# The softmax scaling of the mixers' attention maps moved from VectorE to GpSimd

## The chip, the cores and the metric

The kernel runs on one core of one Trainium2 chip. The core has five engines that run at the same time and wait for each other with semaphores: TensorE (PE, matrix products; its weight loads are shown apart as PEld), VectorE (DVE), ScalarE (ACT), GpSimd (POOL) and SyncE (SP, which issues the DMA transfers). The metric is the device time of the whole program in microseconds (us), the median of several runs.

## The reference

The program is a two-layer backbone over 256 context tokens and 256 latent tokens of width 1024. Each layer is a half-weighted SwiGLU feed-forward part, a mixer, and a second feed-forward part, with modulated RMS norms in front of each. The mixer runs three kinds of heads beside each other on one input projection and joins them in one output projection:

```
# differential heads (4 of them, two maps each)
s1 = q1 @ k1^T * SCALE ; s2 = q2 @ k2^T * SCALE
p  = softmax(s1) - lam * softmax(s2)
o  = rms_norm(p @ v, subln_g) * (1 - lam_init)

# grouped-query heads (4 query heads on 2 key heads)
p  = softmax(q @ k^T)
o  = p @ v

# a bidirectional gated linear recurrence on 256 channels
```

The latent queries attend to all 512 tokens. In the first layer the context queries attend to the 256 context tokens as well; in the last layer the context's outputs aren't needed and are left out. All is in float32.

## The kernel before

Activations are kept transposed, features on the 128 partitions and the 512 tokens along the row. A product of two float32 matrices is made of three TensorE products (`mm3`, lines 375 to 377): each operand is split into a high part (rounded, ScalarE) and a low part (the rest, VectorE, line 369). The two feed-forward parts of each layer take most of the time; the mixers lie at about 410 to 610 us (layer 0) and 1370 to 1530 us (layer 1) of the span.

In the mixer an attention map is computed for 128 queries at a time, queries on the partitions and keys along the row, 256 or 512 of them. `scores` (line 698) has TensorE write the scores to one of three PSUM banks. `softmax` (line 704) has VectorE take the negative maximum of each row (L706), ScalarE the exponential with the row sums as by-product (the call in line 708, shown in the profile as L86, the helper that records it), and VectorE the reciprocal of the sum (L709). The exponentials lie in one of five buffers `e`, the small columns (maximum, sum, reciprocal, scaled reciprocal) in one of eight tiles `sm`.

- In `gqa_att` (line 721) the exponentials are multiplied by the reciprocals (L728) and go to `to_keys`.
- In `da_att` (line 770) there are two maps. The second one's reciprocal is first multiplied by minus lambda (L776), then the second map's exponentials by that (L777), and one instruction scales the first map and adds the second (L778: two tensors in, one out). The sum goes to `to_keys`.
- `to_keys` (line 712) transposes the map in blocks on TensorE (L717) into a single PSUM bank, and ScalarE copies it out (L718). The products with the values follow on TensorE (L734, L783).

Between these steps TensorE works on projections of later heads (`m0vp`, `m0q3p`, `m0k3p` and the like) and on the output projection (`m0oy`), as far as their inputs are there. `rope` (line 521) rotates queries and keys: a shuffle on VectorE (L524), a product with the sine table on GpSimd (L525), one with the cosine table on VectorE (L526), and the sum on VectorE (L527). `stack_q` and `stack_k` split the rotated tensors into their parts (L641, L651, L652 on ScalarE, L642 and L653 on VectorE), `subln` normalises the differential heads (L798 to L804), and `take_m` splits finished heads for the output projection (L790 on ScalarE, L791 on VectorE).

The order of the heads is written in lines 827 to 851. The order of the instructions on each engine is made by a scheduler when the program is built: it takes the instructions by priority as their inputs become ready by its own estimates of durations, and fixes one list per engine. Each engine then works through its list in order, so an instruction that waits holds up all that stand behind it on its engine. GpSimd's list holds little: the rotations, some products of the recurrence (L599), sums of squares (L282) and memsets.

Of the kernel before, what the change touches and what calls it, by code (L numbers as in the profile page):

```python
# [13 lines left out]
ALU = mybir.AluOpType  # L14
# [44 lines left out]
def hybrid_kernel(ctx: ExitStack, tc, x, c, ctx_tok, c_ctx, ada_w, ada_b, norm_g, ffn1_w13, ffn1_w2,  # L59
# [3 lines left out]
    V, S, G, PE = nc.vector, nc.scalar, nc.gpsimd, nc.tensor  # L63
# [32 lines left out]
    def ps(name="ps", tag="ms"):  # L96
        return pss.tile([128, 512], F32, tag=tag, name=name)
# [431 lines left out]
    def mixer(l, c0, nstat):  # L529
        W = w_in[l]  # L530
        nm = f"m{l}"
        with tc.tile_pool(name=f"mp{l}", bufs=1) as mp, tc.tile_pool(name=f"mt{l}", bufs=1) as mt:
            def m512(name, dtype=F32, tag="T"):
                return mt.tile([128, 512], dtype, tag=tag, name=f"{nm}{name}", bufs=TAGS[tag])
# [163 lines left out]
            def scores(q, k, u, a, nk):  # L698
                s = acc_bank(1, "s")
                PE.matmul(s[:, 0:nk], q[u][:, a:a + 128], k[u][:, 0:nk], start=True, stop=False)  # L700
                PE.matmul(s[:, 0:nk], q[u][:, a:a + 128], k[2 + u][:, 0:nk], start=False, stop=True)  # L701
                return s

            def softmax(s, nk, name):
                st_ = sml.tile([128, 4], F32, tag="sm", name="sm", bufs=8)
                V.reduce_max(st_[:, 0:1], s[:, 0:nk], axis=AX.X, negate=True)  # L706
                e = m512(name, tag="e")
                tabled(e[:, 0:nk], s[:, 0:nk], AF.Exp, bias=st_[:, 0:1], accum_out=st_[:, 1:2])
                V.reciprocal(st_[:, 2:3], st_[:, 1:2])  # L709
                return e, st_  # L710

            def to_keys(p, nk):

                tp = ps("tp", "tp")
                pT = m512("pT", tag="p")
                for kt in range(nk // 128):
                    PE.transpose(tp[:, 128 * kt:128 * kt + 128], p[:, 128 * kt:128 * kt + 128], ident)  # L717
                S.activation(pT[:, 0:nk], tp[:, 0:nk], AF.Copy)  # L718
                return pT

            def gqa_att(hp, q0, nk):
                n = nk // 128
                pTs = []
                for qt in range(2):
                    for u in range(2):
                        s = scores(gqa[u], gqa[2], hp, q0 + 128 * qt, nk)
                        e, st_ = softmax(s, nk, "e")
                        V.tensor_scalar(e[:, 0:nk], e[:, 0:nk], st_[:, 2:3], None, op0=ALU.mult)  # L728
                        pTs.append(to_keys(e, nk))
                o = ps("o")  # L730
                for qt in range(2):
                    for kt in range(n):
                        for u in range(2):
                            PE.matmul(o[64 * u:64 * u + 64, 128 * qt:128 * qt + 128],  # L734
                                      gvs[0][:, 128 * kt + 64 * hp:128 * kt + 64 * hp + 64],
                                      pTs[2 * qt + u][:, 128 * kt:128 * kt + 128], start=(kt == 0), stop=(kt == n - 1))
                if 4 + hp not in om:
                    om[4 + hp] = m512(f"og{hp}", tag="o")
                S.activation(om[4 + hp][:, q0:q0 + 256], o[:, 0:256], AF.Copy)
# [30 lines left out]
            def da_att(h, q0, nk):  # L770
                n = nk // 128
                pTs = []
                for qt in range(2):
                    es = [softmax(scores(dq[h], dk[h], u, q0 + 128 * qt, nk), nk, f"e{u}") for u in range(2)]
                    (e1, s1), (e2, s2) = es
                    V.tensor_tensor(out=s2[:, 3:4], in0=s2[:, 2:3], in1=nlam[:, l:l + 1], op=ALU.mult)  # L776
                    V.tensor_scalar(e2[:, 0:nk], e2[:, 0:nk], s2[:, 3:4], None, op0=ALU.mult)  # L777
                    V.scalar_tensor_tensor(e1[:, 0:nk], e1[:, 0:nk], s1[:, 2:3], e2[:, 0:nk], op0=ALU.mult, op1=ALU.add)  # L778
                    pTs.append(to_keys(e1, nk))
                o = ps("o")  # L780
                for qt in range(2):
                    for kt in range(n):
                        PE.matmul(o[:, 128 * qt:128 * qt + 128], vs[h // 2, kt // 2][:, 256 * (kt % 2) + 128 * (h % 2):256 * (kt % 2) + 128 * (h % 2) + 128],  # L783
                                  pTs[qt][:, 128 * kt:128 * kt + 128], start=(kt == 0), stop=(kt == n - 1))
                if h not in om:
                    om[h] = m512(f"o{h}", tag="o")
                S.activation(om[h][:, q0:q0 + 256], o[:, 0:256], AF.Copy)
# [41 lines left out]
            qk_head(1, raw)  # L829
            gqa_proj()  # L830
            attend(da_att, 0)
            attend(da_att, 1)
            gqa_norm()
            ws = v_split(1)
            for t in range(4):
                v_tile(1, ws, t)
            subln((0, 1))
            attend(gqa_att, 0)
            raw = qk_load(1)
            qk_head(2, raw)  # L840
            attend(gqa_att, 1)
            attend(da_att, 2)
            qk_head(3, raw)
            attend(da_att, 3)
# [149 lines left out]
```

## Time and profile before

| | us |
|---|---|
| median of 3 runs | 1734.68 |
| lowest and highest run | 1734.53, 1737.2 |
| the profiled execution | 1734.71 |
| its span in the trace | 1732.9 |

| engine | busy us | share of the span |
|---|---|---|
| TensorE | 1694.8 | 98% |
| VectorE | 1211.4 | 70% |
| ScalarE | 709.6 | 41% |
| GpSimd | 76.4 | 4% |

A busy time counts an instruction from its start to its end. Matmuls are pipelined and their ends are modelled, so short gaps between them do not show. In the rows below a line "L728 DVE" is line 728 on VectorE; "out<-in" names the tiles, with the number of partitions and elements; the share of a slice or window tells how full an engine is while it matters, which the share over the whole span doesn't.

### The profile page before, as it was taken

The numbers are of one execution on the slowest core, as the hardware profiler recorded it, in microseconds if no ns is written. First come the engines' busy times: TensorE is split into PE (matmuls) and PEld (weight loads), VectorE is DVE, ScalarE is ACT, GpSimd is POOL, SyncE is SP. The second block draws the span as 40 slices with busy tenths as digits, with TensorE's granted clock in tenths as the row PEclk, the third lists the DMA queues.
The fourth block names the chain that finished last, engine by engine and source line by source line (L and its number), as shares of the span: only waits on it lengthen the run. The fifth ranks groups of instructions, "written<-read, shape, count | busy, mean of one in ns | idle before, by whom it ended". The sixth has DMA issues, their size and how long they took to land.

```text
span 1732.9 us, 22954 instructions
## 1 busy us (share of the span) xinstructions
PE 1694.8 (98%) x9245; PEld 1440.7 (83%) x9245; DVE 1211.4 (70%) x1863; ACT 709.6 (41%) x1116; POOL 76.4 (4%) x75
## 2 busy tenths in 40 slices
PE   6999999999999999999999999999999999999998
PEld 3788888889787798888888888888888988799997
DVE  5798994337579869999696494563333778987574
ACT  4422222224677743221223342222222477865354
POOL 0000000011101010000000100000001110010001
PEclk9999999999999999999999999999999999999999
DMA  9665752233211147667464344333322332145552
GB/s 347 208 233 203 240 173 98 85 110 104 73 50 50 49 144 245 228 207 244 148 218 163 104 146 146 110 109 98 97 81 90 106 119 74 59 159 179 189 177 92
DMA packets 192817, 249.27 MB, mean 144 GB/s; under 512 B 6722, under 2 KB 170952, under 8 KB 192712
## 3 DMA queue, kind: packets, MB, share of 16 engines
q1 hardware_dynamic: 192712, 247.82, 42.9%
q8 instruction: 72, 1.18, 0.3%
q14 instruction: 33, 0.27, 0.0%
HBM read 246.75 MB, written 1.05 MB: 143 GB/s over the span
## 4 chain that ended last, share of the span: by engine, by line
PE 90%; DVE 6%; ACT 2%; issue 1%; DMA 0%; POOL 0%; SPq 0%; ACTq 0%; DVEq 0%; POOLq 0%
PE f_0pb L377 5%; PE f_0pb L375 5%; PE f_0pb L376 5%; PE f_0pa L376 5%; PE f_0pa L375 5%; PE f_0pa L377 5%; PE f_2pb L376 4%; PE f_2pb L377 4%; PE f_2pa L375 4%; PE f_2pb L375 4%; PE f_2pa L377 3%; PE f_2pa L376 3%; PE f_0w0y L375 3%; PE f_0w0y L377 3%; PE f_0w0y L376 3%; PE f_2w0y L375 2%
## 5 line engine op out<-in xcount | busy, mean ns | idle before, releaser
L227 DVE SCALAR_TENSOR_TENSOR aacc<-araw,cpad,aacc 128x1024 f32<-128x1024 f32 x224 | 276.8, 1279 | 0.0
L86 ACT ACTIVATE g<-f_0pa 128x512 f32<-128x512 f32 x44 | 26.3, 598 | 150.2 <-PE f_0pa L377 150.2
L282 POOL TENSOR_TENSOR sss<-sss,sqs 128x512 f32<-128x512 f32 (+1 forms) x20 | 27.5, 1377 | 1281.5 <-ACT sqs L280 1281.5
L515 DVE TENSOR_TENSOR g<-g,f_0pb 128x512 f32<-128x512 f32 x44 | 30.2, 686 | 68.3 <-PE f_0pb L377 68.0
L369 DVE TENSOR_TENSOR f_0w_0L<-f_0w,f_0w_0H 128x1024 fp32r<-128x1024 f32 (+1 forms) x32 | 34.9, 1090 | 53.5 <-ACT f_0w_0H L368 53.3
L368 ACT ACTIVATE f_0w_0H<-f_0w 128x1024 fp32r<-128x1024 f32 (+1 forms) x32 | 30.5, 952 | 91.9 <-PE f_0w0y L377 43.7
L368 ACT ACTIVATE f_2w_0H<-f_2w 128x1024 fp32r<-128x1024 f32 (+1 forms) x32 | 30.5, 953 | 69.1 <-PE f_2w0y L377 30.7
L369 DVE TENSOR_TENSOR f_2w_0L<-f_2w,f_2w_0H 128x1024 fp32r<-128x1024 f32 (+1 forms) x32 | 34.9, 1089 | 29.1 <-ACT f_2w_0H L368 28.9
L375 PE MATMUL f_0w0y<-f_0gH,f_0w_0H 128*128 128x512 f32 x128 | 50.2, 392 | 0.0
L377 PE MATMUL f_0w0y<-f_0gL,f_0w_0H 128*128 128x512 f32 x128 | 49.9, 390 | 0.0
L376 PE MATMUL f_0w0y<-f_0gH,f_0w_0L 128*128 128x512 f32 x128 | 49.8, 389 | 0.0
L706 DVE TENSOR_REDUCE sm<-s 128x1 f32<-128x512 f32 (+1 forms) x72 | 41.8, 588 | 5.8 <-PE s L701 5.7
L317 ACT ACTIVATE xH<-xn,mods 128x256 fp32r<-128x256 f32 x80 | 35.4, 499 | 25.6 <-DVE xn L316 25.5
L375 PE MATMUL f_2w0y<-f_2gH,f_2w_0H 128*128 128x512 f32 (+1 forms) x128 | 43.2, 338 | 0.0
L377 PE MATMUL f_2w0y<-f_2gL,f_2w_0H 128*128 128x512 f32 (+1 forms) x128 | 43.1, 336 | 0.0
L376 PE MATMUL f_2w0y<-f_2gH,f_2w_0L 128*128 128x512 f32 (+1 forms) x128 | 43.0, 336 | 0.0
L369 DVE TENSOR_TENSOR f_0w_4L<-f_0w,f_0w_4H 128x1024 fp32r<-128x1024 f32 x16 | 19.5, 1221 | 33.0 <-ACT f_0w_4H L368 33.0
L375 PE MATMUL f_0w1y<-f_0gH,f_0w_0H 128*128 128x512 f32 (+1 forms) x120 | 41.7, 348 | 0.0
L376 PE MATMUL f_0w1y<-f_0gH,f_0w_0L 128*128 128x512 f32 (+1 forms) x120 | 41.6, 347 | 0.0
L377 PE MATMUL f_0w1y<-f_0gL,f_0w_0H 128*128 128x512 f32 (+1 forms) x120 | 41.6, 346 | 0.0
L86 ACT ACTIVATE g<-f_2pa 128x512 f32<-128x512 f32 x22 | 13.2, 599 | 68.1 <-PE f_2pa L377 68.1
L368 ACT ACTIVATE f_0w_4H<-f_0w 128x1024 fp32r<-128x1024 f32 x16 | 17.0, 1061 | 58.6 <-PE f_0w0y L377 25.8
(1382 smaller groups left out, 5878.6 us busy)
## 6 DMA issues: line engine op xcount, KB each, us to landing
araw<-in_ada_w_dram SPq DMA_DIRECT2D x64, 1024.0 KB, 4.9
f_0a<-in_ffn_w_dram SPq DMA_DIRECT2D x22, 1024.0 KB, 7.2
f_0b<-in_ffn_w_dram SPq DMA_DIRECT2D x22, 1024.0 KB, 6.1
f_2a<-in_ffn_w_dram SPq DMA_DIRECT2D x22, 1024.0 KB, 7.6
f_2b<-in_ffn_w_dram SPq DMA_DIRECT2D x22, 1024.0 KB, 5.1
f_0w<-in_ffn_w_dram SPq DMA_DIRECT2D x16, 1024.0 KB
f_2w<-in_ffn_w_dram SPq DMA_DIRECT2D x16, 1024.0 KB, 5.3
adas<-in_ada_w_dram SPq DMA_DIRECT2D x16, 512.0 KB, 7.7
```

The costliest lines, as they stand in the source:

```text
L86: i = S.activation(out_, in_, func, **kw)
L227: V.scalar_tensor_tensor(acc[:, v], w[:, i], cpad[:, k, v:v + 1], acc[:, v], op0=ALU.mult, op1=ALU.add)
L282: adder.tensor_tensor(out=self.sum[:, a:b], in0=self.sum[:, a:b], in1=sq[:, a:b], op=ALU.add)
L317: S.activation(xH[:, k, a:b], t[:, a:b], AF.Identity, bias=sh)
L368: S.activation(vH, src, AF.Copy)
L369: V.tensor_tensor(out=vL, in0=src, in1=f32(vH), op=ALU.subtract)
L375: PE.matmul(acc, aH, bH, start=first, stop=False)
L376: PE.matmul(acc, aL, bH, start=False, stop=False)
L377: PE.matmul(acc, aH, bL, start=False, stop=last)
L515: V.tensor_tensor(out=t_[:, c0:], in0=t_[:, c0:], in1=pb[:, c0:], op=ALU.mult)
L706: V.reduce_max(st_[:, 0:1], s[:, 0:nk], axis=AX.X, negate=True)
```

## The change

Two instructions are issued on GpSimd (`G`) instead of VectorE (`V`), with the same operands: the scaling of the grouped-query exponentials, and that of the second differential map.

```
@@ -725,7 +725,7 @@
                     for u in range(2):
                         s = scores(gqa[u], gqa[2], hp, q0 + 128 * qt, nk)
                         e, st_ = softmax(s, nk, "e")
-                        V.tensor_scalar(e[:, 0:nk], e[:, 0:nk], st_[:, 2:3], None, op0=ALU.mult)
+                        G.tensor_scalar(e[:, 0:nk], e[:, 0:nk], st_[:, 2:3], None, op0=ALU.mult)
                         pTs.append(to_keys(e, nk))
                 o = ps("o")
                 for qt in range(2):
@@ -774,7 +774,7 @@
                     es = [softmax(scores(dq[h], dk[h], u, q0 + 128 * qt, nk), nk, f"e{u}") for u in range(2)]
                     (e1, s1), (e2, s2) = es
                     V.tensor_tensor(out=s2[:, 3:4], in0=s2[:, 2:3], in1=nlam[:, l:l + 1], op=ALU.mult)
-                    V.tensor_scalar(e2[:, 0:nk], e2[:, 0:nk], s2[:, 3:4], None, op0=ALU.mult)
+                    G.tensor_scalar(e2[:, 0:nk], e2[:, 0:nk], s2[:, 3:4], None, op0=ALU.mult)
                     V.scalar_tensor_tensor(e1[:, 0:nk], e1[:, 0:nk], s1[:, 2:3], e2[:, 0:nk], op0=ALU.mult, op1=ALU.add)
                     pTs.append(to_keys(e1, nk))
                 o = ps("o")
```

24 instructions of each kind move: in layer 0 sixteen of each (eight with 256 keys, eight with 512), in layer 1 eight of each, all with 512. The scheduler makes new lists from it, so other instructions of the mixers change their places too; SyncE's list stays the same.

VectorE in the first differential heads of layer 0 before: the second maps' scaling (L777) and the sum that uses it (L778), `m0e_3721` and `m0e_3747` being second maps with 512 keys.

```order
L777 TENSOR_SCALAR m0e_3721<-m0e_3721,sm 128x512
L709 RECIPROCAL sm<-sm 128x1
L706 TENSOR_REDUCE sm<-s 128x1
L778 SCALAR_TENSOR_TENSOR m0e_3713<-m0e_3713,sm,m0e_3721 128x512
L776 TENSOR_TENSOR sm<-sm,nlam 128x1
```

The same place of VectorE now, from the scaled reciprocal of the first of these maps on.

```order
L776 TENSOR_TENSOR sm<-sm,nlam 128x1
L709 RECIPROCAL sm<-sm 128x1
L706 TENSOR_REDUCE sm<-s 128x1 x2
L778 SCALAR_TENSOR_TENSOR m0e_3713<-m0e_3713,sm,m0e_3721 128x512
L709 RECIPROCAL sm<-sm 128x1 x2
```

L777 has gone from VectorE's list, and between the scaled reciprocal and the sum stand two maxima here, elsewhere one.

GpSimd in layer 0's mixer: before, the eleven rotation products stand there alone; now the multiplications stand between them. One piece of the difference, from the seventh rotation on.

```order
+L525 TENSOR_TENSOR sh<-sh,cs 128x256 x3
+L728 TENSOR_SCALAR m0e<-m0e,sm 128x256 x3
+L525 TENSOR_TENSOR sh<-sh,cs 128x256
+L728 TENSOR_SCALAR m0e<-m0e,sm 128x256
+L728 TENSOR_SCALAR m0e<-m0e,sm 128x512 x2
+L525 TENSOR_TENSOR sh<-sh,cs 128x256
+L728 TENSOR_SCALAR m0e<-m0e,sm 128x512 x2
+L525 TENSOR_TENSOR sh<-sh,cs 128x256
+L728 TENSOR_SCALAR m0e<-m0e,sm 128x256 x4
```

A rotation now waits in line behind one to three multiplications, each of which waits for a reciprocal from VectorE.

VectorE in layer 0's grouped-query part now, where the rotation and stacking of the next head (`m0qr`, `m0Q`, `kz`) stand among the maxima and reciprocals of the maps.

```order
L706 TENSOR_REDUCE sm<-s 128x1
L642 TENSOR_TENSOR m0Q_4267<-m0qr,m0Q_4267 64x512
L653 TENSOR_TENSOR kz_2951<-m0qr,m0K_4308 64x512
L524 STREAM_SHUFFLE sh<-m0qr 128x256
L526 TENSOR_TENSOR sh<-m0qr,cs 128x256
L369 TENSOR_TENSOR m0o_0_4L<-m0o_0_4819,m0o_0_4H 128x1024
L653 TENSOR_TENSOR kz_2952<-m0qr,m0K_4309 64x512
L709 RECIPROCAL sm<-sm 128x1
L527 TENSOR_TENSOR m0qr<-sh 128x256
```

Before, the same head's instructions stood there with the multiplications L728 between them. L526, L527, L642, L653 and L369 each read two tensors.

## Rows read from the trace of the kernel before

**Rows 1.** The page: busy us of each engine (share of the span) and instructions.
```profile
PE 1694.8 (98%) x9245; PEld 1440.7 (83%) x9245; DVE 1211.4 (70%) x1863; ACT 709.6 (41%) x1116; POOL 76.4 (4%) x75
```

**Rows 2.** The page: the chain of work that ended last, shares by engine.
```profile
PE 90%; DVE 6%; ACT 2%; issue 1%; DMA 0%; POOL 0%; SPq 0%; ACTq 0%; DVEq 0%; POOLq 0%
```

**Rows 3.** VectorE's groups of one shape: xcount | busy us, mean ns | idle before.
```profile
L728 DVE TENSOR_SCALAR m1e<-m1e,sm 128x512 f32<-128x512 f32 x8 | 4.7, 597 | 0.0
L728 DVE TENSOR_SCALAR m0e<-m0e,sm 128x512 f32<-128x512 f32 x8 | 4.2, 535 | 0.0
L777 DVE TENSOR_SCALAR m1e<-m1e,sm 128x512 f32<-128x512 f32 x8 | 3.8, 481 | 0.0
L777 DVE TENSOR_SCALAR m0e<-m0e,sm 128x512 f32<-128x512 f32 x8 | 3.8, 476 | 0.0
L777 DVE TENSOR_SCALAR m0e<-m0e,sm 128x256 f32<-128x256 f32 x8 | 2.8, 345 | 0.0
L728 DVE TENSOR_SCALAR m0e<-m0e,sm 128x256 f32<-128x256 f32 x8 | 2.7, 343 | 0.0
```

**Rows 4.** Mixer windows: width, busy us of PE, PEld, DVE, ACT, POOL; clock; DMA.
```profile
540.00:580.00 40.00, 36.73 (x244) 26.00 (x242) 36.80 (x105) 36.72 (x91) 3.12 (x4) 1.00 0.01 2
1460.00:1520.00 60.00, 57.12 (x392) 47.43 (x392) 53.37 (x125) 46.82 (x97) 5.62 (x7) 1.00 0.28 89
```

**Rows 5.** TensorE's waits, 540 to 580 us: us in total, times, longest.
```profile
PE o L783 <- ACT m0pT L718: 1.6, 2, 0.9
PE m0oy L375 <- ACT xH L790: 1.0, 1, 1.0
PE s L700 <- ACT m0e L86: 0.3, 1, 0.3
```

**Rows 6.** GpSimd's groups of one shape, columns as in rows 3.
```profile
L525 POOL TENSOR_TENSOR sh<-sh,cs 128x256 f32<-128x256 f32 x22 | 19.2, 875 | 211.6 <-DVE sh L524 190.1 <-DVE sm L776 16.0 <-DVE sm L709 5.6
L599 POOL TENSOR_TENSOR m0r<-m0r,m0xc 128x512 f32<-128x512 f32 x4 | 5.1, 1274 | 20.0 <-ACT m0r L86 20.0
L633 POOL MEMSET kz<- 64x512 f32 x8 | 4.2, 521 | 0.4
L554 POOL MEMSET bd<- 128x1024 f32 x2 | 1.9, 955 | 35.2 <-DVE srs L252 35.2
```

**Rows 7.** Layer 0 near 547 us: start us, us, engine, instruction [idle before].
```profile
545.04 0.44 DVE L524 STREAM_SHUFFLE sh<-m0qr 128x256 f32<-128x256 f32 x1
545.38 1.34 DVE L728 TENSOR_SCALAR m0e<-m0e,sm 128x512 f32<-128x512 f32 x2
545.63 0.81 POOL L525 TENSOR_TENSOR sh<-sh,cs 128x256 f32<-128x256 f32 x1 [12.55 <-DVE sh L524]
547.30 0.47 DVE L728 TENSOR_SCALAR m0e<-m0e,sm 128x512 f32<-128x512 f32 x1
547.69 0.41 DVE L526 TENSOR_TENSOR sh<-m0qr,cs 128x256 f32<-128x256 f32 x1
548.62 0.76 POOL L525 TENSOR_TENSOR sh<-sh,cs 128x256 f32<-128x256 f32 x1 [2.18 <-DVE sh L524]
548.70 0.95 DVE L526 TENSOR_TENSOR sh<-m0qr,cs 128x256 f32<-128x256 f32 x1
```

**Rows 8.** Layer 1 near 1481 us, columns as in rows 7.
```profile
1481.07 0.76 POOL L525 TENSOR_TENSOR sh<-sh,cs 128x256 f32<-128x256 f32 x1 [1.93 <-DVE sh L524]
1481.15 0.68 DVE L706 TENSOR_REDUCE sm<-s 128x1 f32<-128x512 f32 x1
```

**Rows 9.** VectorE's row maxima, columns as in rows 3.
```profile
L706 DVE TENSOR_REDUCE sm<-s 128x1 f32<-128x512 f32 x48 | 32.3, 677 | 2.6 <-PE s L701 2.5
L706 DVE TENSOR_REDUCE sm<-s 128x1 f32<-128x256 f32 x24 | 9.5, 410 | 3.3 <-PE s L701 3.2
```

More of the change, by code (lines that the diff above doesn't have):

```diff
@@ L727, in gqa_att @@
                         e, st_ = softmax(s, nk, "e")
-                        V.tensor_scalar(e[:, 0:nk], e[:, 0:nk], st_[:, 2:3], None, op0=ALU.mult)
+                        G.tensor_scalar(e[:, 0:nk], e[:, 0:nk], st_[:, 2:3], None, op0=ALU.mult)
                         pTs.append(to_keys(e, nk))
@@ L776, in da_att @@
                     V.tensor_tensor(out=s2[:, 3:4], in0=s2[:, 2:3], in1=nlam[:, l:l + 1], op=ALU.mult)
-                    V.tensor_scalar(e2[:, 0:nk], e2[:, 0:nk], s2[:, 3:4], None, op0=ALU.mult)
+                    G.tensor_scalar(e2[:, 0:nk], e2[:, 0:nk], s2[:, 3:4], None, op0=ALU.mult)
                     V.scalar_tensor_tensor(e1[:, 0:nk], e1[:, 0:nk], s1[:, 2:3], e2[:, 0:nk], op0=ALU.mult, op1=ALU.add)
```

## The prediction

> **What bounds the kernel now.** I read the busy times first. TensorE is busy 98% of the span, VectorE 70%, ScalarE 41%, GpSimd 4% [rows 1]: nearly all of the time is TensorE's own work, which the change leaves alone. The chain that ended last says the same, 90% TensorE and 6% VectorE [rows 2]. So the change is worth what it does to TensorE's idle time in the two mixers, and nothing elsewhere.
>
> Next, the lines that move. The 48 multiplications take 4.7 + 4.2 + 3.8 + 3.8 + 2.8 + 2.7 = 22.0 us of VectorE: 11.6 us in the grouped-query part (L728: 6.9 in layer 0, 4.7 in layer 1), 10.4 us for the second map (L777) [rows 3]. 22 us is 1.3% of the span, but it is VectorE's time, not TensorE's.
>
> Then the stretches where these lines crowd. From 540 to 580 us (layer 0's grouped-query part and the head after it) VectorE is busy 36.80 of 40 us, ScalarE 36.72, and TensorE idles 3.27. From 1460 to 1520 us (layer 1, a longer stretch) VectorE is busy 53.37 of 60, ScalarE 46.82, and TensorE idles 2.88 [rows 4]. Both helpers are nearly full in layer 0, so an emptied VectorE finds ScalarE next. TensorE's waits in layer 0's stretch all end on ScalarE: on the copy of the transposed map (1.6 us), on a part of the output projection's input (1.0), on an exponential (0.3) [rows 5]. These are late partly because VectorE fed them late, so part of the idle time, not all, is VectorE's to give back. The visible idle time of the two stretches, 3.27 + 2.88 = 6.15 us, is my upper end for a gain. TensorE's spans overlap and hide small gaps, so it is not a strict limit.
>
> **The price of one multiplication on GpSimd.** No row of before shows it. From below, GpSimd's memset, which reads nothing, takes 521 ns for 512 elements and 955 for 1024, so some 0.30 us for 256. From above, its multiplication of two tensors takes 1274 ns for 512 elements; its 256-element one averages 875 [rows 6] and takes 0.76 to 0.81 where it runs in the mixers [rows 7]. The operation added here reads one tensor and a column, so it should lie between; I take 0.90 us for 512 and 0.53 for 256, the middle of the two ends. The 16 short and 32 long ones (the context stream's maps are 256 wide, in layer 0 alone) then make 16 x 0.53 + 32 x 0.90 = 37 us of GpSimd, from 21 to 53 at the ends. GpSimd has that time: it is busy 3.12 of the 40 us [rows 4].
>
> By the Trainium skill, GPSIMD Engine Reference, section 4.1, elementwise work belongs on VectorE, GpSimd being about twice as slow with two inputs and roughly at line rate with one; its section 3.1 gives 769 ns for 512 elements in a tight loop. No row here shows that figure; with it the forecast below would fall by about half a microsecond.
>
> **The grouped-query part, step by step.** Removed: 11.6 us of VectorE. Added: on VectorE nothing, but GpSimd stands in its way. While GpSimd multiplied for 0.76 us from 548.62, VectorE's L526 (two tensors read) took 0.95 us, against 0.41 a microsecond earlier with GpSimd idle; the two L728 around 545.6 took 1.34 together [rows 7], against two times 0.47. So an instruction that meets a running GpSimd loses about 0.5 us. The maxima L706 don't: one ran beside GpSimd at 1481.15 in 0.68 us [rows 8], its usual 677 ns [rows 9].
>
> The Trainium skill (SBUF — State Buffer, "Who interferes with whom") says why the two differ: a VectorE instruction with two tensors in SBUF, or in a two-port mode, shares a port pair with GpSimd, and whoever comes first holds it for the whole instruction; a reduction doesn't. The rows agree. By that rule only the two-tensor instructions below can be hit, and it is the rule that speaks against this change.
>
> In the order of the changed kernel 12 such instructions (L526, L527, L642, L653, L369, L791) stand among layer 0's grouped-query maxima and 13 in layer 1. GpSimd would be busy there about 0.56 of the time (layer 0: 8 x 0.53 + 8 x 0.90 + 3 rotations of 0.8 = 13.9 of some 24.5 us). 25 x 0.56 x 0.5 = 7.0 us; some three of these, 1.4 us, are L526 that meet their own rotation today, as the one at 548.70 did. New: 5.6. VectorE's net relief is 11.6 - 5.6 = 6.0 us. The longer way from the reciprocal through GpSimd to the transpose (0.90 plus two handovers of about 0.1, against 0.47) is covered as long as TensorE has the scores and projections of m0k3 and m1k3 in between; both orders run three to four maps ahead there. Without that cover it would be 24 x 0.5 = 12 us.
>
> GpSimd's queue gets a new neighbour: the rotation products L525 now stand between the multiplications, and VectorE's L527 waits for each. Behind L527 stand the maxima. A rotation that comes behind one or two multiplications is 0.5 to 1.8 us later; L706 and L709 stand in between and take about that, so I cost it at nothing, and at up to 7 x 0.5 us if they don't cover it.
>
> **The differential part.** Removed: 24 L777, 0.48 us (512) or 0.35 (256) each [rows 3]. Added: L778 now waits for GpSimd, with VectorE's next maxima and reciprocals queued behind it, and ScalarE's next exponentials waiting for those. The handover from VectorE to GpSimd takes about 0.15 us (L524 ends at 545.48, L525 starts at 545.63) [rows 7]; I take 0.1 each way. Between the scaled reciprocal L776 and L778 the order leaves one maximum, 0.68 or 0.41 us [rows 9]. For 512: 0.1 + 0.90 + 0.1 - 0.68 = 0.42 of waiting for 0.48 removed; for 256: 0.73 - 0.41 = 0.32 for 0.35. Net 16 x 0.06 + 8 x 0.03 = 1 us of relief, as good as nothing. The ends: with GpSimd at 0.52 and 0.30 the waits are 0.04 and 0.09, relief 16 x 0.44 + 8 x 0.26 = 9 us; at 1.27 and 0.80 they are 0.79 and 0.59, and VectorE loses 16 x 0.31 + 8 x 0.24 = 7 us.
>
> **The sum.** VectorE gains 6.0 + 1 = 7 us. How much of it reaches TensorE? At full conversion 7, at none 0. Layer 0's ScalarE, 92% busy, can give at most 3.28 us before it is the bound itself [rows 4], and the first differential heads of each layer run beside the value projections, where relief buys nothing. I take a bit over a third: 2.5 us. 1734.7 (the profiled execution; its span is 1732.9, with 1.8 around it, and it equals the median of 1734.68) - 2.5 = **1732.2 us**, 0.15% less. I call anything within 0.2% (3.5 us) the same, about what a measurement of this kernel can tell.
>
> **Rivals.**
> 1. GpSimd is slow, and the change costs time. Place: L778 in the differential part. At the two-tensor price VectorE loses 7 us there; in the grouped-query part GpSimd is busy (8 x 0.80 + 8 x 1.27 + 2.4) / 24.5 = 0.77 of the time and holds the port for longer, 25 x 0.77 x 0.7 = 13.5 less the 1.4, against 11.6 removed: another 0.5 lost. Of 7.5 us a bit over half reaches TensorE, more than in the forecast because the chain itself is then longer: +4, 1738.7 us. It decides from about 1.1 us for 512 elements, where the differential part's wait exceeds what was removed by 0.14 us and the port eats the rest. For it: the only multiplications that GpSimd does now run at that price [rows 6]. Against it: they read two tensors. Chance 0.25.
> 2. GpSimd is near its memset price, and VectorE gets 11.6 - 2.5 + 9 = 18 us back; TensorE then loses its visible idle time, 6.15 us: 1728.6. For it: one input, one output, no table. Against it: ScalarE's 92%. Chance 0.27.
> 3. The order, not the price, decides. With VectorE thought lighter, the projection of m0k3 is spread over the grouped-query part and into the next head, and the last differential head's stacking (L653) comes behind five L791 and an L369 on VectorE. TensorE has output projection work there, some 30 matmuls before the next scores. If that covers, it is worth nothing; this and relief that ScalarE absorbs give 1734.7. Chance 0.08, within "same".
>
> **Chances and range.** The forecast, some relief, little of it on the path, has 0.40. Its own spread, 1730 to 1734.5, reaches under the bound of 3.5 us in a fifth of it. Faster: 0.27 + 0.08 = 0.35. Slower: 0.25, rival 1. Same: the rest, 0.40. Range: 1727.5 to 1738.5, to just beyond rival 2 and just short of rival 1's full price.
>
> **What would show it.** L728 and L777 on GpSimd near 0.9 us for 512 elements: right; above 1.1 or under 0.65: rival 1 or 2. VectorE's busy time down by about 15 us rather than 22, with L526, L642 and L653 longer than now. Waits of L778 on GpSimd near 0.4 us. TensorE's idle time in the layer 0 stretch down from 3.3 to about 2, still ended by ScalarE's copies; if instead TensorE's transposes wait for GpSimd, the cover of the longer chain was missing and I am wrong.

## The result, and the profile after

The changed kernel takes 1755.25 us (median, 1753.31 to 1755.62) against 1734.61 in the same job. The ratio is 1.0107, 95% interval 1.0096 to 1.0119: slower, where 1732.2 was forecast, and beyond the range's end of 1738.5. Where a run below is put in us against before, that is its ratio's distance from 1, times 1735; the change costs 18.6 us by it (the two medians alone are 20.6 us apart). The profiled execution has a span of 1753.1 us.

Begin with the same two lines of the page as before. First the busy times, which answer to [rows 1].

```profile
PE 1698.9 (97%) x9245; PEld 1441.6 (82%) x9245; DVE 1199.0 (68%) x1815; ACT 710.2 (41%) x1116; POOL 145.6 (8%) x123
```

VectorE is relieved, by 12.4 us, and TensorE is busy 4.1 us longer, while the span grows by 20.2: the time is idle time of TensorE. The chain that ended last answers to [rows 2].

```profile
PE 84%; DVE 9%; POOL 2%; ACT 2%; issue 2%; DMA 0%; SPq 0%; ACTq 0%; POOLq 0%; DVEq 0%
```

TensorE's share has fallen by 6 points; VectorE has risen by 3 and GpSimd has come in with 2. So less work on VectorE, and more of the chain through it: that is a queue that waits, not one that is full. Next come the lines that moved, on GpSimd now (they answer to [rows 3, 6]; columns as there).

```profile
L777 POOL TENSOR_SCALAR m1e<-m1e,sm 128x512 f32<-128x512 f32 x8 | 13.7, 1716 | 28.5 <-DVE sm L709 14.9 <-DVE sm L776 10.6 <-ACT m1e L86 1.7
L728 POOL TENSOR_SCALAR m0e<-m0e,sm 128x512 f32<-128x512 f32 x8 | 13.2, 1669 | 0.9 <-DVE sm L709 0.9
L777 POOL TENSOR_SCALAR m0e<-m0e,sm 128x512 f32<-128x512 f32 x8 | 13.1, 1631 | 12.7 <-DVE sm L776 4.2 <-DVE sm L709 2.8 <-ACT m0pT L718 2.4
L728 POOL TENSOR_SCALAR m1e<-m1e,sm 128x512 f32<-128x512 f32 x8 | 12.6, 1585 | 8.1 <-DVE sm L709 8.0
L777 POOL TENSOR_SCALAR m0e<-m0e,sm 128x256 f32<-128x256 f32 x8 | 7.4, 923 | 34.7 <-DVE sm L776 28.4 <-ACT m0pT L718 3.5 <-DVE sm L709 2.8
L728 POOL TENSOR_SCALAR m0e<-m0e,sm 128x256 f32<-128x256 f32 x8 | 7.3, 922 | 7.2 <-DVE sm L709 7.2
```

The price is 1585 to 1716 ns for 512 elements and 922 for 256, beyond the upper ends of 1.27 and 0.80 us, and the total is 67.3 us of GpSimd where 37 was taken. Now who waits for it: VectorE's waits at L778 (us in total, times, longest), which before did not exist.

```profile
DVE m0e L778 <- POOL m0e L777: 14.7, 15, 1.8
DVE m1e L778 <- POOL m1e L777: 10.6, 8, 1.8
```

That is 25.3 us in which VectorE stands still, in exchange for 10.4 us of removed work in the same part. And who waits for VectorE: TensorE's transposes, over the whole run. Before, these were all its waits at L717:

```profile
PE tp L717 <- DVE m1e L778: 0.2, 1, 0.2
PE tp L717 <- DVE sm L709: 0.2, 1, 0.2
```

Now they sum to 17.4 us, of the 20.2 by which the span grows; the largest groups, and the direct waits for GpSimd:

```profile
PE tp L717 <- DVE sm L709: 5.4, 8, 1.5
PE tp L717 <- DVE m1e L778: 4.3, 4, 1.4
PE tp L717 <- DVE m0e L778: 4.2, 5, 1.5
...
PE tp L717 <- POOL m1e L728: 1.0, 2, 0.7
...
PE tp L717 <- POOL m0e L728: 0.6, 2, 0.4
```

Most of it ends on VectorE, which itself was waiting. The release named as a reciprocal (L709) can't be a reciprocal's work of 0.16 us; the time line shows one case, in layer 1's second differential head: GpSimd, then VectorE, then TensorE around 1465 us.

```profile
1464.19 1.56 POOL L777 TENSOR_SCALAR m1e<-m1e,sm 128x512 f32<-128x512 f32 x1 [1.22 <-DVE sm L776]
```

```profile
1463.00 0.75 DVE L778 SCALAR_TENSOR_TENSOR m1e<-m1e,sm,m1e 128x512 f32<-128x512 f32 x1 [1.76 <-POOL m1e L777]
1463.67 0.15 DVE L709 RECIPROCAL sm<-sm 128x1 f32<-128x1 f32 x1
1463.86 0.16 DVE L776 TENSOR_TENSOR sm<-sm,nlam 128x1 f32<-128x1 f32 x1
1465.79 0.75 DVE L778 SCALAR_TENSOR_TENSOR m1e<-m1e,sm,m1e 128x512 f32<-128x512 f32 x1 [1.76 <-POOL m1e L777]
```

```profile
1464.96 0.28 PE L376 MATMUL m1vp<-m1v_0H,xL 128*128 128x256 f32 x1
1466.68 0.63 PE L717 MATMUL tp<-cs,m1e 128*128 128x128 f32 x4 [1.44 <-DVE m1e L778]
```

L776 ends at 1464.02, GpSimd starts 0.17 us later, takes 1.56, and L778 starts at once: VectorE idles for the full 1.76 us with nothing between, twice in a row, and TensorE stops at the transposition for 1.44 us, although value projections (`m1vp`), which need nothing of it, stand behind it in its list. The windows of [rows 4], now:

```profile
540.00:580.00 40.00, 37.83 (x249) 27.73 (x248) 30.56 (x81) 32.71 (x86) 27.19 (x22) 1.00 0.08 28
1460.00:1520.00 60.00, 52.83 (x370) 43.80 (x370) 43.46 (x103) 41.40 (x87) 24.83 (x20) 1.00 0.16 54
```

In 540 to 580 us TensorE idles 2.17 us, near the forecast of 2, but that is a coincidence: everything lies some 5 us later than before, so the stretch no longer holds the same work. In 1460 to 1520 it idles 7.17 where it idled 2.88. Layer 0's mixer (from its first projection to the next part's first) grows from 227.6 to 236.5 us, 5.3 of these 8.9 before the third head's projection, that is in the first two differential heads; layer 1's grows from 168.8 to 178.3, 4.2 of it in its first two. In these two stretches VectorE waits 6.0 and 5.8 us at L778, and none of the grouped-query maps is scaled there. Between the mixers it is 1.4 us.

### The profile page after: what moved, and what is told of

Its sections match the earlier page's. It is cut to its first block, busy times and chain, and to the rows that moved or that the text cites. A ratio compares the mean times of both kernels' runs of the same rounds, so it can differ in the third digit from the quotient of the medians.

```text
span 1753.1 us, 23028 instructions
## 1 busy us (share of the span) xinstructions
PE 1698.9 (97%) x9245; PEld 1441.6 (82%) x9245; DVE 1199.0 (68%) x1815; ACT 710.2 (41%) x1116; POOL 145.6 (8%) x123
## 3 DMA queue, kind: packets, MB, share of 16 engines
HBM read 246.75 MB, written 1.05 MB: 141 GB/s over the span
## 4 chain that ended last, share of the span: by engine, by line
PE 84%; DVE 9%; POOL 2%; ACT 2%; issue 2%; DMA 0%; SPq 0%; ACTq 0%; POOLq 0%; DVEq 0%
PE f_0pb L375 5%; PE f_0pb L376 5%; PE f_0pb L377 5%; PE f_0pa L376 5%; PE f_0pa L375 5%; PE f_0pa L377 5%; PE f_2pb L376 3%; PE f_2pb L377 3%; PE f_2pa L375 3%; PE f_2pb L375 3%; PE f_2pa L377 3%; PE f_2pa L376 3%; PE f_0w0y L375 3%; PE f_0w0y L377 2%; PE f_0w0y L376 2%; PE f_2w0y L375 2%
## 5 line engine op out<-in xcount | busy, mean ns | idle before, releaser
L369 DVE TENSOR_TENSOR f_0w_0L<-f_0w,f_0w_0H 128x1024 fp32r<-128x1024 f32 (+1 forms) x32 | 34.9, 1090 | 53.5 <-ACT f_0w_0H L368 53.3
L369 DVE TENSOR_TENSOR f_2w_0L<-f_2w,f_2w_0H 128x1024 fp32r<-128x1024 f32 (+1 forms) x32 | 34.8, 1089 | 29.4 <-ACT f_2w_0H L368 29.2
L317 ACT ACTIVATE xH<-xn,mods 128x256 fp32r<-128x256 f32 x80 | 35.4, 499 | 25.4 <-DVE xn L316 25.3
L369 DVE TENSOR_TENSOR f_0w_4L<-f_0w,f_0w_4H 128x1024 fp32r<-128x1024 f32 x16 | 19.5, 1221 | 33.0 <-ACT f_0w_4H L368 33.0
L86 ACT ACT_TABLE_LOAD x27 | 34.6, 1283 | 10.9 <-PE f_0pa L377 7.5
```

The costliest lines, as they stand in the source:

```text
L86: i = S.activation(out_, in_, func, **kw)
L317: S.activation(xH[:, k, a:b], t[:, a:b], AF.Identity, bias=sh)
L369: V.tensor_tensor(out=vL, in0=src, in1=f32(vH), op=ALU.subtract)
```

## The experiments

Theory A: the loss is VectorE, in order, waiting at L778 for a long GpSimd instruction, with TensorE's transposes behind it. Theory B: it is the shared port, GpSimd slowing VectorE. Theory C: it is the newly made order. Theory D: it is the handing over as such.

### Each half of the change alone, and GpSimd beside an unchanged kernel

The first two undo one of the two lines each. The third keeps both on VectorE and lets GpSimd do as much beside them for nobody.

```
gqa_only   L777: G.tensor_scalar -> V.tensor_scalar
da_only    L728: G.tensor_scalar -> V.tensor_scalar
port_only  both V, and behind each:
+  G.tensor_scalar(d[:, 0:nk], cs[:, C_COS:C_COS + nk], r, None, op0=ALU.mult)   # d is not read
```

> Only the grouped-query scaling (L728) is on GpSimd; the second differential map is scaled on VectorE as before. Theory A (the longer instruction is waited for: 1.56 us for 512 elements on GpSimd against 0.48): the chain to the transpose is longer here too, but three to four maps run ahead, so most of it is covered: 1735 to 1740 us. Theory B (GpSimd holds the port that VectorE's two-tensor instructions need): half of the 48 instructions, so half of the loss, about 1745. Theory C (the newly made lists are bad in themselves): can't say which half, 1735 to 1750.

> Only the second differential map (L777) is scaled on GpSimd. Theory A: VectorE's L778 waits some 1 us for each of the 24, 25 us in all as in the changed kernel, and TensorE's transposes wait behind it: most of the loss is here, 1746 to 1752 us. Theory B: half of the loss, about 1745. Theory C: 1735 to 1750.

> All multiplications stay on VectorE, and beside each one GpSimd multiplies a constant table by the same column into a tile that nobody reads (48 instructions of the same shapes; they are extra work, nothing is left out). Nobody waits for the result, so only the port and the place in GpSimd's queue in front of the rotations are left. Theory A: 1735 to 1739 us. Theory B: the loss of the changed kernel or more, since VectorE's own multiplications are hit as well: 1750 to 1760.

The grouped-query half takes 1740.59 us, ratio 1.0027 [1.0017, 1.0036], +4.7 us. The differential half takes 1754.8, 1.0106 [1.0091, 1.0121], +18.4: nearly the whole loss. The two sum to more than the change (23 us, though the intervals overlap); why is not known. The port alone: 1741.79, 1.0032 [1.002, 1.0044], +5.6, with 74 us of GpSimd. TensorE, VectorE and ScalarE work through the same lists as before there, so this is the price of GpSimd's work beside them, its port and its queue, and of no other order. It slows VectorE's multiplications (here L782, in place of the 476 and 481 ns of [rows 3]):

```profile
L782 DVE TENSOR_SCALAR m0e<-m0e,sm 128x512 f32<-128x512 f32 x8 | 4.8, 601 | 0.0
L782 DVE TENSOR_SCALAR m1e<-m1e,sm 128x512 f32<-128x512 f32 x8 | 4.7, 591 | 0.0
```

And it costs nothing where the change loses 5.3 and 4.2 us. The stretch of the first two differential heads goes from the layer's first projection (in layer 0 at 405.7 us before, 405.9 in `port_only`, 405.4 in the changed kernel) to the third head's, which starts so, in the same order of kernels:

```profile
L375 PE MATMUL m0q2p<-xH,m0q2H x8: 389/389/396, 520.2 to 524.9; 128*128 128x512 f32 x8
L375 PE MATMUL m0q2p<-xH,m0q2H x8: 389/389/396, 520.4 to 525.2; 128*128 128x512 f32 x8
L375 PE MATMUL m0q2p<-xH,m0q2H x8: 389/389/396, 525.2 to 530.0; 128*128 128x512 f32 x8
```

It takes 114.5, 114.5 and 119.8 us; in layer 1 98.6, 98.7 and 102.8. So B is real and too small, and in these heads it is nothing, although all 12 of their GpSimd products run there. In the differential half alone, VectorE's waits are there nearly in full:

```profile
DVE m0e L778 <- POOL m0e L777: 13.5, 15, 1.8
DVE m1e L778 <- POOL m1e L777: 10.8, 8, 1.8
```

18.4 us of loss for 24.3 of wait. All three times lie above what A forecast for them, by 0.6 to 2.8 us, so the wait at L778 is not the whole. In the grouped-query half TensorE waits for GpSimd itself, which the prediction had named as the sign that the cover is missing:

```profile
PE tp L717 <- POOL m1e L728: 2.5, 3, 1.0
PE tp L717 <- POOL m0e L728: 1.9, 3, 0.9
```

### Taking the wait away: order, a tie, another engine

All four with GpSimd or ScalarE have L728 on VectorE, and L777 elsewhere. The first three change the order, the last the engine.

```
da_early   second map's softmax and L777 written ahead of the first map's softmax
da_late    4 softmaxes and both L777 first, then both sums and transpositions (late_v: same, L777 on V)
da_dep     da_late, and the first sum's scale tied to the second tile's reciprocal (dep_v: same, on V):
+  V.scalar_tensor_tensor(s1[:, 3:4], s2[:, 2:3], 0.0, s1[:, 2:3], op0=ALU.mult, op1=ALU.add)
act_da     L777: S.activation(e2[:, 0:nk], e2[:, 0:nk], AF.Copy, scale=s2[:, 3:4])
```

> As da_only, but the second map's softmax and its scaling are written before the first map's, so that the first map's maximum, exponential and reciprocal lie between the scaling on GpSimd and the sum L778 that needs it. Theory A: the wait of L778 falls to under 0.3 us each and the time to 1734 to 1740 us. Theory B: as da_only, since the port is held as long. Theory C: another order, unknown, 1735 to 1750.

> L728 on VectorE as before; L777 on GpSimd as in the change, but both query tiles' four softmaxes and both scalings are written ahead of the two sums and their transpositions, so that GpSimd has a whole softmax of cover for its first tile. Theory A (VectorE waits in order for the long instruction): the waits at L778 fall well below the 24.3 us of the run in which only this line is on GpSimd, to 5 to 10 us, and the time lies within 5 us of the same order with the multiplication on VectorE. Theory B (port): the waits go but the time stays near 1750, since GpSimd runs just as long beside VectorE. If the scheduler again puts the sum close behind, the waits stay near 20 us and so does the time, as with the second map written first.

> The control for the order: four softmaxes first, then two sums and transpositions, with every multiplication on VectorE as in the kernel before. Theory A and B: the order by itself costs little, 1733 to 1740. If it takes more than 1745 the order is what costs in the run beside it, and that run then says nothing of GpSimd.

> As the run with four softmaxes first and L777 on GpSimd, but the first query tile's sum takes its scale from a column that also reads the second tile's reciprocal, so that it can't be put ahead of it (one more instruction on one column, a product with zero, for each pair of tiles). GpSimd runs as often and as long as there. Theory A (VectorE waits in order): the waits of the 12 first tiles go, those of the 12 second tiles stay, 10 to 13 us in all, and the time falls by about 0.75 us for each us of wait, to 1744 to 1747. Theory B (the port): GpSimd's overlap with VectorE is unchanged and so is the time, 1752 to 1755.

> The control for that tie: the same order and the same extra column, with the multiplication on VectorE. Both theories: 1735 to 1739; what it has above the kernel before is the price of the order, and is taken off the run beside it.

> L728 on VectorE as before; L777 on ScalarE as a copy with a scale column (its copies of 512 columns take 0.6 us). The same handing over to another engine as in the change, without GpSimd's duration and without its port. The long instruction (theory A): VectorE's wait at L778 falls to about 24 x 0.7 = 17 minus what stands between, some 8 us or less, and the time is 1735 to 1741. The handing over as such (theory D): 1745 to 1755, as with GpSimd.

Writing things in another order did not move the wait much, since the scheduler put the sum close behind GpSimd again: `da_early` 1749.54, 1.0078 [1.0063, 1.0093], with 19.5 us of waits; `da_late` 1753.45, 1.0102 [1.0086, 1.0117], with 22.7. Both missed the hoped-for covered wait, but they tell of the order: `late_v`, written the same with the product on VectorE, is 0.9999 [0.999, 1.0008]. Writing it so costs nothing. The lists that the scheduler makes of the two differ, though, so this control doesn't settle C; `spread` below does. The tie did move the wait. Its waits (L778 is line 781 there):

```profile
DVE m0e L781 <- POOL m0e L777: 5.5, 6, 1.4
DVE m1e L781 <- POOL m1e L777: 4.2, 5, 1.4
```

They are 9.7 us, and GpSimd's instructions are as long as ever (1857 and 1828 ns). `da_dep` takes 1747.03, 1.0062 [1.0049, 1.0076], +10.8; its control `dep_v` 1740.8, 1.0025 [1.0015, 1.0034], +4.3 (above its forecast of 1735 to 1739), the price of the tie, again with lists of its own. Against the controls the loss falls from 17.9 us (`da_late`) to 6.5 (`da_dep`) as the wait falls from 22.7 to 9.7: 0.79 and 0.67 us for each us of wait, with GpSimd as busy beside VectorE in the one as in the other. B forecast no change here, and falls as the main cause.

On ScalarE, where the product takes 0.72 us for 512 columns, the waits are 3.7 us and the time is 1739.44, 1.0017 [1.0008, 1.0026], +2.9: a handing over that is short costs little, which speaks against D.

```profile
DVE m1e L778 <- ACT m1e L777: 1.9, 3, 0.9
DVE m0e L778 <- ACT m0e L777: 1.8, 4, 0.8
```

### The duration

`half` is the changed kernel with only half of each row's columns scaled; `spread` scales whole rows, with the product written as one of two tensors.

```
half    G.tensor_scalar(e2[:, 0:nk // 2], e2[:, 0:nk // 2], s2[:, 3:4], None, op0=ALU.mult)        (L728 likewise)
spread  G.tensor_tensor(out=e2[:, 0:nk], in0=e2[:, 0:nk], in1=s2[:, 3:4].to_broadcast([128, nk]), op=ALU.mult)
        (L728 likewise; spread_gqa: L728 alone, L777 on V)
```

> The changed kernel, in which GpSimd scales only the first half of each row's columns (the other half stays unscaled), so that its instruction is shorter and nothing else moves. The long instruction (theory A): for 512 columns GpSimd now takes 0.92 us, as the trace of the changed kernel shows for rows of 256, instead of 1.56 to 1.7; the 25.3 us that VectorE waits at L778 fall to about 24 x (1.8 - 0.65)/2, some 8 to 12 us, and the time comes to 1738 to 1745. The shared port (theory B): the overlap halves, and so does that part of the loss: GpSimd beside VectorE cost 6.5 us in the run that kept the order, which would leave 3; the wait itself would not matter. The handing over as such (theory D: what costs is one more change of engine in each chain, whatever its length): the time stays at 1752 to 1756.

`half`: 1741.93, 1.0035 [1.0024, 1.0046], +6.1, with 13.5 us of waits, its products of 256 columns at 958 to 1065 ns. The time is as A said, and the wait as its sum gives, which is 13.8 us and not the 8 to 12 written behind it; D said 1752 to 1756. The expectation has nothing else move, but the scheduler made other lists, so this run doesn't separate duration from order. Why the whole row is so slow was then asked of GpSimd itself, by five forms in turn beside the kernel before, run once for its rows alone:

```
forms   f == 0: G.tensor_scalar(d, c, r, None, op0=ALU.mult)        f == 1: G.tensor_scalar(d, c, 0.5, None, op0=ALU.mult)
        f == 2: G.tensor_copy(d, c)                                 f == 3: G.tensor_tensor(out=d, in0=c, in1=c, op=ALU.mult)
        else:   G.tensor_tensor(out=d, in0=c, in1=r.to_broadcast([128, 512]), op=ALU.mult)
```

> Every multiplication stays on VectorE; beside each, GpSimd runs one of five forms in turn on 512 columns of a constant table into a tile that nobody reads, 9 or 10 of each: a product with a column (the change's form), a product with a constant, a copy, a product of two tensors, and a product of a tensor with the column spread over the row. What is open is why the change's form took 1.56 us and more, where the prediction put the two-tensor product's 1.27 us as the upper end. If the column operand is what costs: column form 1.6 to 1.8, constant 0.9 to 1.1, copy 0.6 to 0.9, two tensors 1.2 to 1.4, spread column as two tensors. If it is this part of the program (VectorE beside it): all forms lie together at 1.5 to 1.8, the two-tensor product too.

Its groups on GpSimd, with the column (L729), with a constant (L731), the copy (L733), two tensors (L735), the spread column (L737):

```profile
L731 POOL TENSOR_SCALAR bd<-cs 128x512 f32<-128x512 f32 x11 | 17.9, 1628 | 0.7
L729 POOL TENSOR_SCALAR bd<-cs,sm 128x512 f32<-128x512 f32 x9 | 15.5, 1724 | 17.4 <-DVE sm L709 16.8 <-DVE sm L795 0.5
L737 POOL TENSOR_TENSOR bd<-cs,sm 128x512 f32<-128x512 f32 x9 | 9.7, 1081 | 69.4 <-DVE sm L709 44.9 <-DVE sm L795 24.4
L735 POOL TENSOR_TENSOR bd<-cs 128x512 f32<-128x512 f32 x9 | 9.4, 1048 | 0.8
L733 POOL COPY bd<-cs 128x512 f32<-128x512 f32 x10 | 6.9, 691 | 0.6
```

Neither expectation holds: the place is not it, since the two-tensor product takes 1.05 us here, and the column is not it, since a constant is as slow. It is the form: a tensor with a scalar takes half as long again as a product of two tensors. Written as two tensors, with the same column, the change's product should be cheaper:

> The changed kernel, with both GpSimd multiplications written as a product of two tensors, the second being the column spread over the row (a stride of nothing). The probe beside this took 1.05 us for 512 columns in that form, where the changed kernel's form took 1.57. If the loss is the duration (theory A): the waits of VectorE at L778 fall from 25.3 us to about 24 x (1.05 - 0.5) = 13, as in the run with half the columns (13.5 us, 6.7 us slower than before), and the time is 1740 to 1744. If the loss has another cause: it stays at 1750 or more.

> Only the grouped-query multiplication on GpSimd, in the form with the spread column; the differential part as before. With the slow form this half of the change cost 4.7 us. VectorE is relieved of 11.6 us there; with the map scaled 0.5 us sooner, TensorE's 4.4 us of waits for it should go to 1 or 2: 1733 to 1738. Faster than the kernel before if the relief is worth what the next run shows.

`spread` takes 1741.35, 1.0035 [1.0022, 1.0049], +6.1, where the changed kernel has +18.6. Its products of the second map, and VectorE's waits for them:

```profile
L777 POOL TENSOR_TENSOR m1e<-m1e,sm 128x512 f32<-128x512 f32 x8 | 9.3, 1164 | 28.5 <-DVE sm L709 14.8 <-DVE sm L776 11.9 <-ACT m1e L86 1.7
...
L777 POOL TENSOR_TENSOR m0e<-m0e,sm 128x512 f32<-128x512 f32 x8 | 8.3, 1040 | 12.9 <-DVE sm L776 5.5 <-DVE sm L709 2.8 <-PE m0k3p L377 1.9
...
L777 POOL TENSOR_TENSOR m0e<-m0e,sm 128x256 f32<-128x256 f32 x8 | 4.9, 613 | 34.6 <-DVE sm L776 29.8 <-DVE sm L709 2.8 <-ACT m0pT L718 2.0
```

```profile
DVE m0e L778 <- POOL m0e L777: 5.6, 7, 1.2
DVE m1e L778 <- POOL m1e L777: 5.3, 6, 1.2
```

14.4 us less of waiting, 12.5 us less of time. Read side by side, the traces of `spread` and of the changed kernel have the same instructions in the same order on TensorE, VectorE, ScalarE and GpSimd. So these 12.5 us are none of C's: two thirds of the loss was that form, through its duration. (GpSimd is also 22 us less busy, which at the rate of `port_only` is some 1.7 us, an estimate.) In the first two differential heads, where the port cost nothing, the stretches are 2.9 and 2.2 us shorter than in the changed kernel for 3.3 and 2.2 us less of wait: nearly a us of time for each. (In layer 0 `spread` has its first projection at 404.9 us and the third head's at 521.8.)

And yet, at a price of 1.04 to 1.16 us, somewhat above the 0.90 that the prediction took, the change still loses. The grouped-query half alone in this form is 1737.87, 1.0014 [1.0005, 1.0022], +2.4, with the lists of `gqa_only` and 2.8 us of transposes waiting for GpSimd where that has 4.4: still no gain.

### What the relief was worth

Three kernels take the multiplications off VectorE without a price on GpSimd, and one makes one of them smaller.

```
none      L728 and L777 left out (the maps stay unscaled)       none_gqa   L728 left out, L777 on V
fold      L777 gone, and the first maps' reciprocals with it:
+  V.scalar_tensor_tensor(s2[:, 3:4], s2[:, 2:3], nlam[:, l:l + 1], s1[:, 1:2], op0=ALU.mult, op1=ALU.mult)
+  V.scalar_tensor_tensor(e1[:, 0:nk], e2[:, 0:nk], s2[:, 3:4], e1[:, 0:nk], op0=ALU.mult, op1=ALU.add)
diag_v    L728 as a 128x128 diagonal, and the transposition as a matmul with it:
+  V.tensor_scalar(dg, ident, st_[:, 2:3], None, op0=ALU.mult)
+  PE.matmul(tp[:, ...], p[:, ...], dg, start=True, stop=True)
```

> Both multiplications are left out altogether, on VectorE and on GpSimd: the maps stay unscaled (the differential sum then subtracts nothing scaled by lambda). This gives the whole of what taking them off VectorE could bring, with no price on GpSimd. The prediction credited the relief with 11.6 us of VectorE in the grouped-query part and 10.6 us in the differential part, and with a bit over a third of what is left of it: by that conversion 1735 - 22.2 x 0.4 = 1726 or so. Rival (the relief was never on the path, since TensorE's stream is full there): 1733 to 1736.

> The grouped-query maps stay unscaled (L728 is left out), the differential part is as before: what taking 11.6 us off VectorE there could bring at the most. Leaving out both brought 5.3 us, folding the differential one 0.8. If the relief counts in the grouped-query part alone: 1730 to 1732. If the two are only worth something together: 1734 to 1736.

> No multiplication on GpSimd, and L777 is gone instead of moved: the sum becomes e1 + c e2 in one VectorE instruction with c = -lambda r2 sum1, so its result is the old one times the first map's sum. The normalization over the features behind it divides that factor out again (but for its small constant under the root). The first maps' reciprocals fall away too (24 of 0.15 us). VectorE does 24 x 0.44 + 24 x 0.15 = 14 us less. By what leaving both multiplications out brought for 22 us (6 us, that is 0.27 for each us): 1732, ratio 0.998. If all of that gain came from the grouped-query part: 1735 to 1737. If all came from the differential part: 1729 to 1731.

> Neither multiplication is on GpSimd. In the grouped-query part VectorE multiplies no map: it scales the 128 x 128 identity by the reciprocals (a quarter of the elements of a 512-column map), and the transposition is a matmul of the map with that diagonal, so the scaling comes with it. The differential part is as before. Theory A: what the change was to relieve is VectorE's 32 multiplications; if this relief is worth the net 6 us that the prediction gave it, and a third to a half of it reaches the end, the time is 1731 to 1733; if TensorE's matmul with a diagonal takes longer than its transposition (four passes instead of one), each of 112 costs up to 0.3 us more, and the time comes to 1740 to 1765. Theory B says nothing different.

`none` takes 1730.96, 0.9965 [0.9952, 0.9979], -6.1: all that was to be had, for 22 us of instructions (VectorE's busy time falls by 16.4). `none_gqa`: 1732.74, 0.9982 [0.9973, 0.9991], -3.1. Both lie between the times forecast for them. `fold`: 1735.68, 0.9996 [0.9987, 1.0005]: 14 us of instructions taken out of the differential part for nothing measurable. Its expectation of 1732 missed, and it doesn't beat the kernel before. `diag_v`: 1739.53, 1.0021 [1.0013, 1.003], +3.6, also a miss. A matmul takes no longer there than a transpose, 284 and 277 ns against 276, but each of the 80 blocks (the expectation has 112) now stands in the trace as two matmuls, 160 where there were 80, and their weight loads take 191 ns where the transposes' take 141. TensorE's busy time grows by 8.2 us, which is enough for the loss; that it is the loss was not tried.

## Why the prediction was wrong

**The price.** Taken at 0.90 us for 512 columns with 1.27 as the upper end; measured 1.59 to 1.72, and 0.92 for 256 instead of 0.53. The bound rested on the operation's form: it "reads one tensor and a column, so it should lie between" a memset and a two-tensor product. The probe shows this false on GpSimd: the form, not the number of tensors read, sets its time. Rival 1 was the right one in place and direction, and its own price was too low for the same reason: it gave 4 us of loss. Its 1.1 us as the point from which the change loses doesn't hold either, since at 1.04 to 1.16 us it already costs 6.1 (`spread`). (At 0.77 us the prediction's own terms lower its sum by about 0.9 us, an estimate, and not by the half that it states.)

**The step that fails near the predicted price too** is the netting in the differential part: "0.42 of waiting for 0.48 removed", and so in all "1 us of relief, as good as nothing". A wait and a removed instruction are not the same microsecond. Removing 14 us of instructions there gave 0.7 us, not clear of nothing (`fold`); a us of waiting at L778 cost 0.67 to 0.79 (`da_dep`, `da_late`, their share of the port included), and 0.87 between `spread` and the changed kernel. At 1.04 to 1.16 us the waits are 10.9 us for 10.4 removed, which the netting calls nothing, and the kernel is 6.1 us slower, 2.4 of it in the grouped-query half alone. No run had 0.90 itself. VectorE has slack on average, so work taken from it was mostly hidden already; but a wait falls in the one chain (reciprocal, product, sum, transposition) that TensorE's list stands behind.

**The cover** of "one maximum, 0.68 or 0.41 us" between L776 and L778 was taken for every place. In the changed order it stands there for 14 of the 24 sums, and for only 6 of the 16 with 512 keys. With the formula of the prediction (0.1 + 1.56 + 0.1, less 0.68 where it stands), 6 x 1.08 + 10 x 1.76 + 8 x 0.71 = 29.8 us; the trace has 25.3. The formula was fair, its count of covers was not: the last four sums of layer 1 have no maximum. Where nothing at all stands between, at four places, the wait is 1.76 to 1.79 us; at the other six without a maximum some other VectorE instruction stands there and shortens it.

**The conversion.** "A bit over a third" for relief was not far off: 6.1 of 22 us, 0.28 (`none`), with 3.1 of 11.6 in the grouped-query part. That relief in the first differential heads buys nothing was right: with the products left out (`none`) their stretches take 114.4 and 99.0 us, against 114.5 and 98.6. For the later ones it is open, as `none` is 3.0 us faster than `none_gqa`, but `fold` gained nothing clear. That a loss there costs as little was the silent second half of that sentence, and wrong: 5.3 of layer 0's 8.9 us and 4.2 of layer 1's 9.6 were lost in the stretch of just those heads. Rival 1's "a bit over half" was nearer, still short of the 0.7 to 0.9.

**The grouped-query part.** Forecast: 6.0 us of net relief, a third of it gained, the longer way to the transposition covered by TensorE's other work. Measured: +4.7 us alone, with 4.4 us of transposes waiting for GpSimd: the cover holds only in part. The port's price there, 5.6 us of VectorE, was set too high: layer 0's rotation and stacking of the differential heads (L526, L527, L642, L653 on `m0qr`) took 19.8 us before and 20.3 after, and VectorE's busy time is no longer with L728 on GpSimd than without it (1204.0 us in `gqa_only`, 1204.8 in `none_gqa`). For the whole change it fell by 12.4 us where leaving the products out lets it fall by 16.4, so by this the port costs all of VectorE about 4 us. The rotations that stand behind GpSimd's products, put at nothing, cost a little: VectorE's waits for them at L527 grew from 0.9 to 3.8 us.

**What held.** The handover, 0.17 us by the trace where 0.1 was taken, and that TensorE's own work would hardly change (1694.8 to 1698.9 us). GpSimd's time as such cost less (5.6 us in `port_only`, where VectorE's own products are hit as well) than the waiting for it. VectorE's busy time fell by less than was removed (12.4 us, about 15 forecast), but mostly by luck: without any product on GpSimd (`none`) it falls by only 16.4 of the 22.0, as VectorE's instructions overlap at their ends in the trace (above, L709 starts before L778 of 1463.00 has ended), and the port has but 4 of the rest.

**Open.** Why the two halves, +4.7 and +18.4, give 18.6 together. How much of the remaining 6.1 us of `spread` is port, how much wait and how much its order. Whether a covered wait in both query tiles would bring the differential part to even: no tie for the second tile was tried.

## What to carry to other kernels

Price a moved instruction by its own form on the engine it goes to, and where no row shows that form, treat the upper end as unknown rather than as the next dearer-looking row. Don't net a new wait against removed work: a us of work on an engine with slack was worth a quarter of a us here, a us of wait in a chain that TensorE's list stands behind cost 0.7 to 0.9. Count what stands between a handing over and the instruction that waits for it at every place of the new order, and ask first what leaving the work out altogether would gain; here that was 6 us at best, and every way of moving it lost 2 to 19.

## What the runs showed of the hardware

- GpSimd, 512 float32 columns on 128 partitions, at the shortest in the probe: a tensor with a column 1.57 us, with a constant 1.49, two tensors 1.04, a column spread over the row 1.04, a copy 0.61. The slow rows of the kernel before ([rows 6], 1274 ns for two tensors) were not the floor of that form, and the scalar form, which reads less, is the slowest.
- GpSimd beside VectorE lengthens VectorE's products of a tensor with a column, from 476 to 601 ns (`port_only`), and its two-tensor sum at L778 from 744 to 819; row maxima stay at 675 to 679 ns, 677 before. The Trainium skill (SBUF — State Buffer, "Who interferes with whom") gives this division, and the trace agrees.
- The Trainium skill (GPSIMD Engine Reference, section 4.1) has GpSimd roughly at line rate with one input. The copy at 0.61 us fits that, beside VectorE's product at 0.48 us; the product with a scalar at 1.5 to 1.7 us doesn't: the measurement decides.
